# A hybrid decoder step: the MLP's down-projection computed by Strassen's seven products, like its up-projection

## The chip, the cores and the metric

The kernel runs on one core of a Trainium2 chip. The metric is the device time of one execution in microseconds. Five engines share the core's on-chip memory SBUF: TensorE (PE, matmuls into PSUM), VectorE (DVE), ScalarE (ACT), GpSimd (POOL) and SyncE (SP, which here only issues DMAs). Each runs its own instructions strictly in the order of the program; semaphores make one wait for another.

## The reference, cut to what matters

One layer on 1024 prompt tokens and 8 sample tokens (1032 columns in the kernel), with model width 1024 and MLP width 4096, in float32:

```python
def hybrid_layer(x, p, ...):
    ...
    x = x + jnp.concatenate([o, sg.astype(x.dtype)], axis=-1) @ w_out
    x = x + jnp.square(jax.nn.relu(rms_norm(x, g_ff) @ w_up)) @ w_down
    x = x + (p @ w_ple) * jax.nn.sigmoid(rms_norm(x, g_ple) @ w_ple_gate)
    return x, new_hist, s_new.astype(x.dtype), vg
```

The change concerns the second line's `@ w_down` and what follows it: the norm before the gate needs the sum of squares of each whole column of the new x.

## The kernel before, in words

Activations are kept transposed: 128 rows of the model width by 1032 tokens, so X1 is eight tiles. Every float32 product is three passes of a rounded format: a value is split into `hi` (a cast on ACT, line 147) and `lo` (a subtraction on DVE, line 150), and PE computes hi·hi, lo·hi and hi·lo. `form` (line 157) makes the split weight of one 128x512 group in a ring of four (`wsp`).

The up-projection already uses Strassen's algorithm: the two halves of the model width, of the hidden units and of each half of the tokens give 2x2 blocks, and seven products P1 to P7 of sums of blocks replace eight. `xform` makes the seven sums of the activations once and keeps them in FB. `up_stage` runs 16 pairs of hidden units, seven products each, each for two halves of the tokens with 12 matmuls of 258 columns (line 1175), and joins the products at their eviction from PSUM (lines 1186 to 1197). `hidden` takes relu and the square, splits the result (ACT 1206 and 1209, POOL 1210, DVE 1211) and writes it to DRAM (h_d, line 1212).

The down-projection is straight. `down` takes groups of two or four blocks of 128 hidden units (DBLK), loads their split activations back from h_d (`load_h`), and for each of eight output blocks and three token blocks (384, 384 and 264 columns) runs 3 matmuls per hidden block (lines 196 to 198). `evd` multiplies the PSUM sum by the norm's factor rr on DVE (line 1338) and adds it into X1 on POOL (line 1340). In the last group the addition is on DVE, `split_gain` (ACT 153, DVE 154) makes the gate's split input, and `add_ss` squares on ACT (line 1309) and adds to the sum of squares ss on POOL (line 1310).

Then the gate: PE's order is written by generators (`weave` and `spawn`, with modelled times). `gate_units` runs the matmuls for token blocks 0 and 1, then 2; beside them `p_in` transposes the per-layer input (pT, lines 1372 to 1374), and `rows` takes the column sums of ss by matmuls against ones (ms, line 1106), the inverse root on DVE, one transpose (msT, line 1123) and a way through DRAM (row_d) to rr. Evictions of the gate are held until that row is there. `first_out` writes the chunks of 128 tokens of the first two blocks while the third runs; the last three chunks (6, 7 and the sample tokens) are normed and written after it.

PE and SP have an order written out by hand in the down stage; ACT, DVE and POOL are put in order by a scheduler with its own estimates when the kernel is built.

Of the kernel before, what the change touches and what calls it, by code (L numbers as in the profile page):

```python
# [17 lines left out]
P = 128  # L18
# [14 lines left out]
HB = NT // 4  # L33
QBLK = [(i * HB, HB) for i in range(4)]

STEPS = (("P1", 0, "A", True), ("P4", 6, "C", True), ("P5", 3, "D", True), ("P6", 5, "A", False),
         ("P7", 4, "B", True), ("P2", 2, "A", True), ("P3", 1, "D", False))
FREE = [x[1] for x in STEPS]

# [3 lines left out]
DBLK = (2, 2, 4, 4, 4, 4, 4, 4, 4)  # L43
# [38 lines left out]
def trunk_step_kernel(  # L82
# [62 lines left out]
    def split(dst_hi, dst_lo, src, hi_eng, lo_eng):  # L145
        if hi_eng is S:
            S.copy(dst_hi, src)  # L147
        else:
            hi_eng.tensor_copy(dst_hi, src)
        lo_eng.tensor_sub(dst_lo, src, f32(dst_hi))  # L150

# [112 lines left out]
    h_d = dram.tile([32, P, 2, NT], F32, name="h_d")  # L264
# [6 lines left out]
    with ExitStack() as mix:  # L271
# [469 lines left out]
        def gdn_out(h, z):  # L741
# [18 lines left out]
            for o, w in BLK:  # L760
                b = slice(o, o + w)
                split(RA[8 + 2 * h][:, b], RA[9 + 2 * h][:, b], z[:, b], S, V)
# [235 lines left out]
        with tc.manual_schedule(engines={mybir.EngineType.PE}):  # L998
# [13 lines left out]
            for o, w in BLK:  # L1012
                for h in range(NH):
                    split(RA[2 * h][:, o : o + w], RA[2 * h + 1][:, o : o + w], us[h][:, o : o + w], S, V)
# [5 lines left out]
            for m in range(KD):  # L1020
                SY.dma_start(X1[m], xfm_d[m])
# [39 lines left out]
        fst = ctx.enter_context(pool("fst"))  # L1061
        FB = fst.tile([P, 14, 8 * HB], F32R, name="fb")
        Q = fst.tile([P, 8, HB], F32, name="q8")

        def xform(k, tp):

            H2 = HB // 2
            cells = FB[:, 7 * tp : 7 * tp + 7, :]
            for s in range(2):
                q = Q[:, 4 * s : 4 * s + 4, :].rearrange("p a (b c) -> p (a b) c", b=2)  # L1070
                with tc.high_priority(2 * PRI):
                    for i in range(2):
                        x = X1[k + 4 * i][:, 2 * HB * tp : 2 * HB * tp + 2 * HB].rearrange("p (a b) -> p a b", a=2)
                        S.activation(q[:, 2 * i : 2 * i + 2], x[:, :, H2 * s : H2 * s + H2],
                                     AF.Copy, scale=gff[:, k + 4 * i : k + 4 * i + 1])
                    G.tensor_sub(q[:, 4:6], q[:, 0:1].to_broadcast([P, 2, H2]), q[:, 1:3])
                    G.tensor_sub(q[:, 6], q[:, 2], q[:, 4])
                    G.tensor_sub(q[:, 7], q[:, 3], q[:, 6])  # L1078
                    hi = cells[:, :, HB * k + H2 * s : HB * k + H2 * s + H2]
                    lo = cells[:, :, HB * (k + 4) + H2 * s : HB * (k + 4) + H2 * s + H2]  # L1080
                    S.copy(hi, q[:, 1:8])  # L1081
                    V.tensor_sub(lo, q[:, 1:8], f32(hi))
# [13 lines left out]
    x1p = ctx.enter_context(pool("x1p", side="right"))  # L1096
    rr = x1p.tile([P, NT], F32, name="rr")

    def tok_stat(ss, power, chunks=range(NU + 1), more=None):
# [4 lines left out]
        for c in chunks:  # L1104
            r = P if c < NU else TS
            PE.matmul(ps[:r, c : c + 1], lhsT=ss[:, c * P : c * P + r], rhs=ones[:, 0:1], start=True, stop=not more)
            if more:
                d = (c - more[1]) * P
                PE.matmul(ps[:r, c : c + 1], lhsT=more[0][:, d : d + r], rhs=ones[:, 0:1], start=False, stop=True)
        tok_power(tok, ps, power, chunks, more)  # L1110
        return tok

    def tok_power(tok, ps, power, chunks, fast=None):
        c0, c1 = chunks[0], min(chunks[-1] + 1, NU)
        V.tensor_scalar(tok[:, c0:c1], ps[:, c0:c1], 1.0 / D, EPS, op0=ALU.mult, op1=ALU.add)
        if chunks[-1] == NU:
            V.tensor_scalar(tok[:TS, 8:9], ps[:TS, 8:9], 1.0 / D, EPS, op0=ALU.mult, op1=ALU.add)
        if power != 1:
            (rsqrt_act if fast else rsqrt)(tp, tok[:, :], tok[:, :], "rp")

    def row_stat(tok, out, i, ps):

# [4 lines left out]
        SY.dma_start(out, row_d[i, :NT].partition_broadcast(P))  # L1127
# [4 lines left out]
    th = ust.enter_context(pool("th", 2, side="right"))  # L1132
# [27 lines left out]
    def up_stage():  # L1160
        source = up_forms()
        forms = [next(source) for _ in range(RING)]
        for p in range(16):
            bank, u1, u2, u3 = {}, {}, {}, {}
            turn = TURN if p else TURN0
            for n, (i, t) in enumerate(turn):
                name, f, b, first = STEPS[i]
                wh, wl = forms[7 * p + i]
                if first:
                    bank[b, t] = pu.tile([P, 512], F32, tag=f"{b}{t}", name=b)[:, :HB]  # L1170
                ps = bank[b, t]
                x = FB[:, 7 * t + f, :].rearrange("p (j k c) -> p j k c", j=2, c=HB)
                for k in range(4):
# [3 lines left out]
                    if k < 3:  # L1177
                        yield 3 * HB * 0.000455
                if (i, t) not in turn[n + 1 :] and (i, 1 - t) not in turn[n + 1 :]:
                    forms += [w for w in (next(source, None),) if w]  # L1180
                q = Q[:, 4 * t : 4 * t + 4, :]
                with tc.high_priority(PRI):
                    if name == "P1":
                        u1[t] = tp.tile([P, HB], F32, tag="u1", name="u1")
                        S.copy(u1[t], ps)
                    elif name == "P6":
                        u2[t] = tp.tile([P, HB], F32, tag="u2", name="u2")
# [322 lines left out]
```

## Time and profile before

| | us |
|---|---|
| median of 3 runs (least to greatest) | 1430.12 (1429.49 to 1434.62) |
| the profiled execution: time, span of its instructions | 1426.78, 1425.1 |
| PE busy in the span | 1345.1 (94%) |
| from the end of the up-projection to msT | 907.8 to 1301.4 |
| of this, the stretch in which the down-projection runs | 920.1 to 1283.9 |
| gate and output, from msT to the end | 1301.4 to 1425.1 |

The last three rows are stretches on the span's clock, read from the trace. PE is the busiest engine; POOL and DVE are busy about half and six tenths of the span. TensorE's granted clock is given as a share of full speed.

### The profile page before, as it was taken

How to read it: one execution, taken by the hardware profiler on the slowest of the kernel's cores; microseconds unless marked ns; L12 is line 12 of the kernel's file. 1: busy time of each engine (PE TensorE's matmuls, PEld its weight loads, DVE VectorE, ACT ScalarE, POOL GpSimd, SP SyncE). 2: the span in 40 equal slices, each digit the busy share in tenths (PEclk: the TensorE clock that was granted, in tenths of full speed). 3: DMA queues.
4: the chain of work that ended last, by engine and by line, in shares of the span. 5: the costliest groups of instructions: out<-in, count | busy, mean ns of one | idle time of the engine just before them, and what ended most of it. 6: DMA issues, size and time to landing. Idle time of an engine off the chain costs nothing.

```text
span 1425.1 us, 25172 instructions
## 1 busy us (share of the span) xinstructions
PE 1345.1 (94%) x9567; PEld 1316.0 (92%) x9567; DVE 875.1 (61%) x1670; ACT 569.9 (40%) x1248; POOL 711.2 (50%) x798
## 2 busy tenths in 40 slices
PE   6979978989999899899999999699999999999998
PEld 4979968889899899799999999699999999998998
DVE  7745755375937846576776677475445445596346
ACT  6575645532233216555555454311111111154445
POOL 5300988847415306656656444296444445343331
PEclk9999989999999999999999999899999999999999
DMA  7334525555426721254445543674333344211124
GB/s 238 95 90 132 152 78 144 178 153 152 138 75 205 221 66 30 78 161 163 144 157 164 188 152 124 247 267 153 134 135 134 138 153 153 77 45 47 59 60 164
DMA packets 194837, 193.91 MB, mean 136 GB/s; under 512 B 18112, under 2 KB 160651, under 8 KB 190612
## 3 DMA queue, kind: packets, MB, share of 16 engines
q1 hardware_dynamic: 194716, 192.31, 42.0%
q8 instruction: 75, 1.23, 0.4%
q14 instruction: 46, 0.38, 0.1%
HBM read 131.76 MB, written 60.62 MB: 135 GB/s over the span
## 4 chain that ended last, share of the span: by engine, by line
PE 73%; POOL 9%; DVE 7%; DMA 4%; ACT 4%; issue 2%; SPq 0%; DVEq 0%; POOLq 0%; ACTq 0%
PE g L196 14%; PE g L198 14%; PE g L197 14%; PE A L1175 9%; PE D L1175 7%; PE B L1175 3%; PE C L1175 3%; POOL xinv L630 3%; POOL it L629 3%; DVE x L1340 1%; DVE fb L154 1%; DVE wlo L150 1%; POOL q L1078 1%; DMA s<-in_state_gdn 1%; DMA fb<-h_d 1%
## 5 line engine op out<-in xcount | busy, mean ns | idle before, releaser
L196 PE MATMUL g<-fb,whi 128*128 128x384 f32 (+1 forms) x960 | 309.6, 322 | 11.5 <-DMA fb<-h_d 11.0
L197 PE MATMUL g<-fb,wlo 128*128 128x384 f32 (+1 forms) x960 | 308.3, 321 | 0.0
L198 PE MATMUL g<-fb,whi 128*128 128x384 f32 (+1 forms) x960 | 307.7, 320 | 0.0
L196 PE MATMUL g<-ra,whi 128*128 128x384 f32 (+2 forms) x800 | 271.5, 339 | 0.6 <-ACT ra L374 0.6
L198 PE MATMUL g<-ra,whi 128*128 128x384 f32 (+2 forms) x800 | 255.5, 319 | 1.3 <-DVE ra L375 0.6
L197 PE MATMUL g<-ra,wlo 128*128 128x384 f32 (+2 forms) x800 | 254.4, 318 | 0.0
L1340 POOL TENSOR_TENSOR x<-x,t 128x384 f32<-128x384 f32 (+1 forms) x192 | 182.2, 960 | 143.4 <-DVE t L1338 143.3
L147 ACT CAST whi<-st 128x512 fp32r<-128x512 f32 x160 | 98.7, 620 | 349.4 <-PE g L198 336.8
L1338 DVE TENSOR_TENSOR t<-g,rr 128x384 f32<-128x384 f32 (+1 forms) x216 | 111.0, 515 | 148.2 <-PE g L198 140.1
L196 PEld LDWEIGHTS g<-fb,whi 128*128 128x128 f32 x960 | 181.5, 189 | 12.8 <-issue 10.3
L150 DVE TENSOR_TENSOR wlo<-st,whi 128x512 fp32r<-128x512 f32 x158 | 148.6, 941 | 61.4 <-ACT whi L147 57.8
L198 PEld LDWEIGHTS g<-fb,whi 128*128 128x128 f32 x960 | 181.4, 189 | 0.0
L197 PEld LDWEIGHTS g<-fb,wlo 128*128 128x128 f32 x960 | 181.4, 189 | 0.0
L196 PEld LDWEIGHTS g<-ra,whi 128*128 128x128 f32 x800 | 153.5, 192 | 2.8 <-ACT ra L374 1.0
L198 PEld LDWEIGHTS g<-ra,whi 128*128 128x128 f32 x800 | 153.1, 191 | 3.1 <-POOL ra L375 2.0
L197 PEld LDWEIGHTS g<-ra,wlo 128*128 128x128 f32 x800 | 153.9, 192 | 0.7 <-DVE wlo L150 0.3
L1175 PE MATMUL A<-fb,whi 128*128 128x258 f32 x768 | 147.8, 284 | 6.0 <-ACT fb L1081 4.6
L1175 PEld LDWEIGHTS A<-fb,whi 128*128 128x128 f32 x768 | 122.7, 190 | 7.0 <-ACT fb L1081 5.0
L1210 POOL TENSOR_TENSOR q<-q 128x516 f32<-128x516 f32 x64 | 69.3, 1086 | 103.4 <-ACT hs L1209 96.8
L1211 DVE TENSOR_TENSOR hs<-q,hs 128x516 fp32r<-128x516 f32 x64 | 87.1, 1360 | 46.8 <-POOL q L1210 46.7
L1175 PE MATMUL A<-fb,wlo 128*128 128x258 f32 x384 | 108.7, 283 | 0.0
L1175 PE MATMUL D<-fb,whi 128*128 128x258 f32 x512 | 98.7, 284 | 0.0
(382 smaller groups left out, 2596.8 us busy)
## 6 DMA issues: line engine op xcount, KB each, us to landing
h_d<-hs SPq DMA_DIRECT2D x64, 516.0 KB
fb<-h_d SPq DMA_DIRECT2D x32, 1032.0 KB
st<-in_w_down SPq DMA_DIRECT2D x32, 512.0 KB
st<-in_w_in SPq DMA_DIRECT2D x24, 512.0 KB
ck<-ck_d SPq DMA_DIRECT2D x32, 320.0 KB
ra<-in_w_up SPq DMA_DIRECT2D x32, 256.0 KB
rb<-in_w_up SPq DMA_DIRECT2D x32, 256.0 KB
st<-in_w_ple_gate SPq DMA_DIRECT2D x16, 512.0 KB
```

The source lines that it names most:

```text
L147: S.copy(dst_hi, src)
L150: lo_eng.tensor_sub(dst_lo, src, f32(dst_hi))
L196: PE.matmul(ps[:, :w], lhsT=whi[k], rhs=xh, start=(k == 0), stop=False)
L197: PE.matmul(ps[:, :w], lhsT=wlo[k], rhs=xh, start=False, stop=False)
L198: PE.matmul(ps[:, :w], lhsT=whi[k], rhs=xl, start=False, stop=(k == nk - 1))
L629: G.tensor_mul(tv, a, x)
L630: G.tensor_sub(X[:, j + 1 :, :w], X[:, j + 1 :, :w], tv)
L1175: PE.matmul(ps, lhsT=a[:, k, :], rhs=x[:, c, k, :], start=(first and k == 0 and j == 0), stop=(k == 3 and j == 2), skip_group_check=True)
L1210: G.tensor_mul(q, q, q)
L1211: V.tensor_sub(v[:, 1], q, f32(v[:, 0]))
L1338: V.tensor_mul(t[:, :w], ps[:, :w], rr[:, o : o + w])
L1340: (V if last else G).tensor_add(xv, xv, t[:, :w])
```

## The change

The hidden activations are no longer split before they go to DRAM. The up-projection's eviction writes relu² of a 2x2 group of blocks, `dforms` makes the other four of the seven sums with three POOL instructions, and two DMAs write the seven unsplit forms to f_d (4 groups of 1024 hidden units by 7 forms). Tokens lie in quarters of 256, 256, 260 and 260 columns for this, so X1 is loaded in three pieces each, and the forms of the up-projection lie in two tiles, which makes the copy and the subtraction of `xform` two instructions each. X1 is saved to x1_d, and its memory, FB's and Q's are given up after the up-projection.

`down` then goes through 4 row groups of w_down by 7 products (DSTEPS gives the order P1, P5, P6, P7, P4, P2, P3). A product is 4 output blocks by 2 halves by 12 matmuls of 256 or 260 columns; its form comes by one load of 1 MB into `raw` and is split by ACT and DVE (`split_raw`), and its weights are quarters of w_down in SBUF, summed on POOL where the product wants a sum, and then split. Seven sums per output block are kept in SBUF (ACC and three more): the first group's products are copied there by ACT, those of the others are added by DVE. In the last group these are joined: 20 additions on POOL and 8 on DVE (`add`), then `finish`: the product with rr on DVE, X1 (reloaded from x1_d) added on POOL, the square on ACT into one tile `sq`, the sum of squares on POOL. The gate's input for quarters 0 and 2 is made as the sums become final; that for quarters 1 and 3, which needs memory of the loop, after it. The gate runs in four blocks, 0 and 2 and then 1 and 3; four chunks are written beside the second pass and five after it. The load of w_ple and of the per-layer input stands after the loop's last activations.

```diff
-DBLK = (2, 2, 4, 4, 4, 4, 4, 4, 4)
+DSTEPS = (("P1", 0), ("P5", 4), ("P6", 5), ("P7", 6), ("P4", 3), ("P2", 1), ("P3", 2))
...
-    h_d = dram.tile([32, P, 2, NT], F32, name="h_d")
+    f_d = dram.tile([4, 7, P, 8 * 258], F32, name="f_d")
+    x1_d = dram.tile([KD, P, NT], F32, name="x1_d")
...
             for m in range(KD):
-                SY.dma_start(X1[m], xfm_d[m])
+                for dst, src in permuted(X1[m], xfm_d[m], 0, NT):
+                    SY.dma_start(dst, src)
...
+        FB = [(fst.tile([P, 4, 4128], F32R, name="fb"), 3), (fst.tile([P, 3, 4128], F32R, name="fa"), 0)]
...
+                    for fb, i0 in FB[::-1]:
+                        hi, lo = fb[:, :, c0 : c0 + h2], fb[:, :, c0 + 4 * w : c0 + 4 * w + h2]
+                        qi = q[:, i0 : i0 + fb.shape[1]]
+                        S.copy(hi, qi)
+                        V.tensor_sub(lo, qi, f32(hi))
...
+                        V.tensor_add(q[:, 3], u2[t], ps)
+                if name in ("P7", "P3"):
+                    for func in (AF.Relu, AF.Square):
+                        v = q[:, 1:3] if name == "P7" else q[:, 0:4:3]
+                        S.activation(v, v, func)
+                if name == "P3":
+                    dforms(p, t, q)
+                yield 3 * w * 0.000455
+    def dforms(p, t, q):
+        w = WT[t]
+        tt = tp.tile([P, 4 * 260], F32, tag="tt", name="tt")[:, : 4 * w].rearrange("p (a b) -> p a b", a=4)
+        G.tensor_sub(tt[:, 1:4:2], q[:, 3:4].to_broadcast([P, 2, w]), q[:, 0:3:2])
+        G.tensor_sub(tt[:, 2], q[:, 2], tt[:, 1])
+        G.tensor_sub(tt[:, 0], q[:, 1], tt[:, 2])
+        c0 = 1024 * t + w * (p % 4)
+        SY.dma_start(f_d[p // 4, 0:3, :, c0 : c0 + w].rearrange("f p c -> p f c"), q[:, 0:3])
+        SY.dma_start(f_d[p // 4, 3:7, :, c0 : c0 + w].rearrange("f p c -> p f c"), tt)
...
+        for m in range(KD):
+            SY.dma_start(x1_d[m], X1[m])
+            yield 3.0
...
+    ACC = pacc.tile([P, 2, 2, 4, 516], F32, name="acc")
+    ss = pacc.tile([P, 2, 516], F32, name="ss")
+    sq = pacc.tile([P, 516], F32, name="sq")
...
+    seq = [(j, i) for j in range(4) for i in range(7)]
...
+    def load_raw(n):
+        if n < len(seq):
+            j, i = seq[n]
+            SY.dma_start(raw, f_d[j, DSTEPS[i][1]])
+    def split_raw(n):
+        if n < len(seq):
+            hi, lo = HC[n % 2]
+            with tc.high_priority(PRI):
+                for c in (slice(0, 1024), slice(1024, 2064)):
+                    S.copy(hi[:, c], raw[:, c])
+                    V.tensor_sub(lo[:, c], raw[:, c], f32(hi[:, c]))
...
+    def down_forms():
+        for j in range(4):
+            sums = dst.tile([P, 4, 4, P], F32, tag="s", name="sums")
+            for name, _ in DSTEPS:
+                for p in range(4):
+                    with tc.high_priority(PRI):
+                        if name == "P5":
+                            G.tensor_add(sums[:, p], a_of("A21", p), a_of("A22", p))
+                        elif name == "P6":
+                            G.tensor_sub(sums[:, p], sums[:, p], a_of("A11", p))
+                        if name in ("P7", "P3"):
+                            f = dst.tile([P, 4, P], F32, tag="t", name="sd")
+                            G.tensor_sub(f, *((a_of("A21", p), a_of("A11", p)) if name == "P7" else (a_of("A12", p), sums[:, p])))
+                        else:
+                            f = {"P1": "A11", "P4": "A22", "P2": "A12"}.get(name)
+                            f = a_of(f, p) if f else sums[:, p]
+                        f = form(f)
+                    yield f
...
+    def finish(ab, nn, p, xo):
+        a = ACC[:, ab, nn, p]
+        V.tensor_mul(a, a, rr[:, nn])
+        G.tensor_add(a, a, xo[:, p])
+        if nn in begun:
+            S.activation(sq, a, AF.Square)
+            G.tensor_add(ss[:, nn], ss[:, nn], sq)
+        else:
+            begun.add(nn)
+            S.activation(ss[:, nn], a, AF.Square)
+    def gate_in(ab, nn, p):
+        m = p + 4 * ab
+        hi, lo = XS[ab, nn]
+        split_gain((hi[:, p], lo[:, p]), ACC[:, ab, nn, p], gple[:, m : m + 1])
...
+    def down():
+        load_raw(0)
+        load_a(0, "A11")
+        split_raw(0)
+        load_raw(1)
+        load_a(0, "A21")
+        load_a(0, "A22")
+        load_a(0, "A12")
+        row_get(rr, 1)
+        source = down_forms()
+        forms = [next(source) for _ in range(RING)]
+        xo = {}
+        for n, (j, i) in enumerate(seq):
+            name = DSTEPS[i][0]
+            split_raw(n + 1)
+            load_raw(n + 2)
+            hs = HC[n % 2]
+            end = j == 3
+            for p in range(4):
+                wh, wl = forms.pop(0)
+                for t in range(2):
+                    w = WT[t]
+                    ps = psd.tile([P, 512], F32, tag="d", name="d")[:, :w]
+                    xh, xl = (h[:, 1024 * t : 1024 * t + 4 * w].rearrange("p (k c) -> p k c", k=4) for h in hs)
+                    for k in range(4):
+                        PE.matmul(ps, lhsT=wh[:, k, :], rhs=xh[:, k, :], start=(k == 0), stop=False)
+                        PE.matmul(ps, lhsT=wl[:, k, :], rhs=xh[:, k, :], start=False, stop=False)
+                        PE.matmul(ps, lhsT=wh[:, k, :], rhs=xl[:, k, :], start=False, stop=(k == 3))
+                    to = {"P2": "P1", "P3": "P6"}.get(name, name) if end else name
+                    a = acc[to][:, p, TOFF[t] : TOFF[t] + w]
+                    with tc.high_priority(PRI):
+                        if j == 0:
+                            S.copy(a, ps)
+                        else:
+                            V.tensor_add(a, a, ps)
+                f = next(source, None)
+                if f:
+                    forms.append(f)
+                if end:
+                    def add(eng, x, y):
+                        eng.tensor_add(acc[x][:, p], acc[x][:, p], acc[y][:, p])
+                    if name == "P6":
+                        add(G, "P6", "P1")
+                        add(G, "P1", "P2")
+                    elif name == "P7":
+                        add(G, "P7", "P6")
+                        add(G, "P6", "P5")
+                        add(V, "P5", "P7")
+                        add(G, "P6", "P3")
+                    elif name == "P4":
+                        add(V, "P7", "P4")
+                        finish(1, 1, p, xo[1, 1])
+                    elif name == "P2":
+                        finish(1, 0, p, xo[1, 0])
+                        gate_in(1, 0, p)
+                    elif name == "P3":
+                        finish(0, 0, p, xo[0, 0])
+                        gate_in(0, 0, p)
+                yield 24 * 258 * 0.000455
+            if not end:
+                for name in {3: ("A11", "A21"), 4: ("A22",), 6: ("A12",)}.get(i, ()):
+                    load_a(j + 1, name)
+            elif i == 3:
+                xo[1, 1] = x1_old("A11", 1, 1)
+                xo[1, 0] = x1_old("A21", 1, 0)
+            elif i == 4:
+                xo[0, 0] = x1_old("A22", 0, 0)
+            elif i == 5:
+                xo[0, 1] = x1_old("A11", 0, 1)
+        for p in range(4):
+            finish(0, 1, p, xo[0, 1])
...
+    for p in range(4):
+        for ab in range(2):
+            gate_in(ab, 1, p)
...
-        weave(gate_units((0, 1), False, None))
...
-        weave(gate_units((2,), True, q7))
+        weave(gate_units((0, 2)))
+        spawn(first_out(), FIN0)
...
+        weave(gate_units((1, 3), [q7]))
```

On POOL at the end of the down-projection, the order before is this (x1 is X1, ss the sum of squares, q a square):

```order
L1340 TENSOR_TENSOR x1_5547<-x1_5547,t_14154 128x384
L1340 TENSOR_TENSOR x1_5547<-x1_5547,t_14170 128x384
L1340 TENSOR_TENSOR x1_5547<-x1_5547,t_14186 128x264
L1310 TENSOR_TENSOR ss_11069<-ss_11069,q_14274 128x384
L1310 TENSOR_TENSOR ss_11069<-ss_11069,q_14295 128x384
```

POOL's last work for the loop is a single addition per eviction, and none of PE's operands are made there. In the changed kernel, this is POOL in the same place, inside the last row group (sd is a sum of weights that PE's products P7 and P3 wait for, acc the sums kept on chip, a11 and a21 old X1 or weights):

```order
L1363 TENSOR_TENSOR sd_14390<-a21_11058,a11_11061 128x512
L1437 TENSOR_TENSOR acc_11027<-acc_11027 128x516
L1437 TENSOR_TENSOR acc_11027<-acc_11027,acc_P2_11040 128x516
L1437 TENSOR_TENSOR acc_11027<-acc_11027 128x516 x2
L1363 TENSOR_TENSOR sd_14737<-a12_11055,sums_13873 128x512
L1437 TENSOR_TENSOR acc_11027<-acc_11027 128x516 x2
L1437 TENSOR_TENSOR acc_11027<-acc_11027,acc_P3_11041 128x516
L1437 TENSOR_TENSOR acc_11027<-acc_11027 128x516 x2
L1437 TENSOR_TENSOR acc_11027<-acc_11027,acc_P3_11041 128x516
L1383 TENSOR_TENSOR acc_11027<-acc_11027,a11_11061 128x516
```

The weight sums of the product P3 stand among the joining additions. Counted from the first of these (the first line with L1437 that the whole order of the last group has), 14 instructions stand before the first sum of P3 (sd_14737), and 43 before its fourth and last.

On ACT where the gate begins, the order before is:

```order
L153 ACTIVATE fb_6085<-x1_5547,vec_149 128x384
L1309 ACTIVATE q_14703<-x1_5547 128x384
L153 ACTIVATE fb_6085<-x1_5547,vec_149 128x264
L1309 ACTIVATE q_14724<-x1_5547 128x264
L1373 CAST fb_6085<-pT_14761 128x384
```

Each square follows its cast, and the casts of the per-layer input come when all squares are done. After (xt is the gate's input of quarters 1 and 3, wpl the split w_ple, pp the per-layer input):

```order
L166 ACTIVATE xt00_15030<-acc_11027,vec_150 128x516
L166 ACTIVATE xt10_15032<-acc_11027,vec_150 128x516
L150 CAST wpl00_15077<-st_15081 128x1024
L150 CAST wpl10_15079<-st_15085 128x1024
L1385 ACTIVATE sq_11029<-acc_11027 128x516 x2
L1543 CAST pp00_15089<-pT_15118 128x256
L1385 ACTIVATE sq_11029<-acc_11027 128x516
L1543 CAST pp10_15091<-pT_15129 128x256
L1385 ACTIVATE sq_11029<-acc_11027 128x516
```

Eight casts of the gate's input (the last two are shown) and two of w_ple now stand before the last six squares, and casts of the per-layer input among these.

## Rows read from the trace of the kernel before

**Rows 1.** The page: the span, and busy time, share and count of each engine.

```profile
span 1425.1 us, 25172 instructions
PE 1345.1 (94%) x9567; PEld 1316.0 (92%) x9567; DVE 875.1 (61%) x1670; ACT 569.9 (40%) x1248; POOL 711.2 (50%) x798
```

**Rows 2.** Busy time by stretch: the start of the down stage, its body, its last group, the wait for the gate's row, and the gate with the output.

```profile
core 0: us, PE busy (x) PEld busy (x) DVE busy (x) ACT busy (x) POOL busy (x), PEclk, DMA share, GB/s
907.80:920.10 12.30, 1.35 (x5) 0.85 (x4) 3.14 (x7) 3.06 (x6) 2.09 (x2) 0.71 0.98 339
920.10:1243.00 322.90, 322.90 (x2045) 322.83 (x2046) 170.00 (x254) 37.79 (x60) 182.24 (x192) 1.00 0.42 156
1243.00:1283.90 40.90, 40.50 (x259) 40.10 (x257) 38.77 (x63) 20.69 (x44) 17.44 (x16) 1.00 0.13 40
1283.90:1301.40 17.50, 14.10 (x75) 12.94 (x74) 13.95 (x33) 7.14 (x17) 5.34 (x5) 0.80 0.11 30
1301.40:1425.10 123.70, 117.61 (x782) 117.12 (x781) 58.34 (x115) 60.01 (x112) 35.23 (x36) 0.99 0.28 90
```

**Rows 3.** The chain that ended last, where the up-projection passes into the down-projection: start, duration, what.

```profile
902.09 2.87 PE A L1175 x24
904.96 2.87 PE D L1175 x24
...
907.85 0.42 DVE q L1197
...
910.35 9.67 DMA fb<-h_d
...
920.07 0.69 PE g L196
```

**Rows 4.** Durations by line on DVE, ACT and POOL: count, then least, median and greatest duration in ns, first and last start.

```profile
L150 DVE TENSOR_TENSOR wlo<-s,whi x64: 676/680/1804, 585.1 to 897.5; 128x512 fp32r<-128x512 f32 x64
L150 DVE TENSOR_TENSOR fb<-st,fb x2: 1226/1524/1823, 941.0 to 943.5; 128x1024 fp32r<-128x1024 f32 x2
L154 DVE SCALAR_TENSOR_TENSOR fb<-x,vec,fb x24: 482/618/1376, 1242.1 to 1293.0; 128x384 fp32r<-128x384 f32 x16, 128x264 fp32r<-128x264 f32 x8
L1195 DVE TENSOR_TENSOR q<-u,A x32: 407/418/424, 599.5 to 905.0; 128x258 f32<-128x258 f32 x32
L1211 DVE TENSOR_TENSOR hs<-q,hs x64: 680/1488/1785, 600.9 to 913.9; 128x516 fp32r<-128x516 f32 x64
L1157 POOL TENSOR_TENSOR s<-rb,s x16: 1276/1291/1747, 591.8 to 895.1; 128x512 f32<-128x512 f32 x16
L153 ACT ACTIVATE fb<-x,vec x24: 499/616/620, 1241.5 to 1291.3; 128x384 fp32r<-128x384 f32 x16, 128x264 fp32r<-128x264 f32 x8
L147 ACT CAST fb<-st x2: 1042/1044/1047, 938.8 to 939.8; 128x1024 fp32r<-128x1024 f32 x2
```

**Rows 5.** The timeline of DVE and of POOL in the up stage: start, duration, instruction.

```profile
706.65 1.68 DVE L1211 TENSOR_TENSOR hs<-q,hs 128x516 fp32r<-128x516 f32 x1
710.85 1.23 DVE L1211 TENSOR_TENSOR hs<-q,hs 128x516 fp32r<-128x516 f32 x1
...
706.47 1.31 POOL L1153 TENSOR_TENSOR s<-rb,ra 128x512 f32<-128x512 f32 x1 [0.63 <-DVE wlo L150]
711.49 1.75 POOL L1157 TENSOR_TENSOR s<-rb,s 128x512 f32<-128x512 f32 x1
```

**Rows 6.** The same at the end of the down stage, and PE's matmuls there (their starts give the time of one).

```profile
1282.24 1.04 POOL L1310 TENSOR_TENSOR ss<-ss,q 128x384 f32<-128x384 f32 x1 [1.91 <-ACT q L1309]
1291.49 2.15 POOL L1310 TENSOR_TENSOR ss<-ss,q 128x384 f32<-128x384 f32 x2 [1.56 <-ACT q L1309]
...
1282.32 1.38 DVE L1340 TENSOR_TENSOR x<-x,t 128x384 f32<-128x384 f32 x1
...
1283.31 0.28 PE L197 MATMUL g<-fb,wlo 128*128 128x264 f32 x1
1283.80 0.28 PE L198 MATMUL g<-fb,whi 128*128 128x264 f32 x1
1292.68 2.41 PE L1106 MATMUL ms<-ones,ss 128*128 128x1 f32 x12 [1.86 <-POOL ss L1310]
1301.37 0.28 PE L1123 MATMUL msT<-ident,tok 128*9 128x128 f32 x1
1302.72 0.34 PE L197 MATMUL g<-fb,wlo 128*128 128x384 f32 x1
1303.25 0.34 PE L197 MATMUL g<-fb,wlo 128*128 128x384 f32 x1
```

**Rows 7.** DMA issues on SP at the start of the down stage, and output halves on ACT and DVE at the end of the program: start, duration, instruction.

```profile
908.39 0.57 SPq L1279 DMA_DIRECT2D st<-in_w_down  x1
...
1419.00 1.82 ACT L1402 ACTIVATE yo<-yT,tok 128x512 f32<-128x512 f32 x3 [0.95 <-DVE tok L252]
...
1420.42 0.64 DVE yo L1404
```

More of the change, by code (lines that the diff above doesn't have):

```diff
@@ L1103, in tok_stat, with row_put @@
         V.memset(tok, 1.0)
[L1104 to L1110, printed above, removed]
-        return tok
[L1113 to L1121, printed above, removed]
+        tok_sums(ps, ss, chunks, more)
+        tok_mean(tok, ps, chunks)
+        (rsqrt_act if more else rsqrt)(tp, tok[:, :], tok[:, :], "rp")
+        return tok
+    def row_put(tok, i, ps):
         PE.transpose(ps[:9, :], tok, ident)
@@ new lines, in trunk_step_kernel @@
+    for name in ("A22", "A21"):
+        AC[name] = dl.tile([P, 2064], F32, name=name.lower())
+    HC[0] = [dl.tile([P, 2064], F32R, name=f"h0{i}") for i in range(2)]
+    AC["A11"] = dl.tile([P, 2064], F32, name="a11")
+    raw = dl.tile([P, 2064], F32, name="raw")
+    seq = [(j, i) for j in range(4) for i in range(7)]
[10 more added lines that the diff above has]
+                    V.tensor_sub(lo[:, c], raw[:, c], f32(hi[:, c]))
@@ L1249, in trunk_step_kernel @@
+    with tc.manual_schedule(engines={mybir.EngineType.PE, mybir.EngineType.SP}):
+        weave(down())
+    dx.close()
+    dlx.close()
+    gst = ctx.enter_context(pool("gst"))
+    XS.update({(ab, 1): [gst.tile([P, 4, 516], F32R, name=f"xt{ab}{i}") for i in range(2)] for ab in range(2)})
+    for p in range(4):
+        for ab in range(2):
+            gate_in(ab, 1, p)
     tp = ctx.enter_context(pool("tp", 3, side="right"))
     wst2 = ctx.enter_context(pool("wst2", side="right"))
-    ss = wst2.tile([P, NT], F32, name="ss")
@@ L1290, in halves @@
             with tc.high_priority(PRI):
-                ready.append([form(x) for x in staged[n]])
+                ready.append([form(staged[n][:, 4 * j : 4 * j + 4, :]) for j in range(2)])
+    stage()
+    stage()
+    halves()
     cur = [0]
@@ L1357, in trunk_step_kernel @@
         SY.dma_start(st, w_ple[0, k * P : (k + 1) * P, :])
-        split(wpl[k][0], wpl[k][1], st[:, :], S, V)
-    pp = [cell(4 + k) for k in range(2)]
+        split(wpl[k][0][:, :], wpl[k][1][:, :], st[:, :], S, V)
+    pp = [[gst.tile([P, 2, 516], F32R, name=f"pp{k}{i}") for i in range(2)] for k in range(2)]
     pt = []
@@ L1443, in rows, with first_out @@
             ev()
-    def first_out(c1):
-        tok = tok_stat(ss, -0.5, range(c1))
+    first, second = (0, 1, 4, 5), (2, 3, 6, 7, NU)
+    def first_out():
+        tok = tok_stat(ss, first)
         yield FIN
-        for c in range(c1):
-            while c >= c1 - LATE and not gated:
+        for c in first:
+            while c == first[-1] and not gated:
                 yield 0.5
```

371 lines of the change are left out of this document (197 added, 174 removed).

## The prediction

> **What bounds the kernel now.** I read the page first: PE is busy 94% of the span, POOL 50%, DVE 61% [rows 1]. The busy time by stretch shows where this holds. In the body of the down stage PE has no idle time at all (322.90 of 322.90 us), beside 170 us of DVE and 182 us of POOL. At its start PE works 1.35 us in 12.3 us, at a granted clock of 0.71 and a DMA share of 0.98; after its end it waits for the sum of squares (14.10 us busy in 17.5 us, clock 0.80) [rows 2]. So fewer matmuls shorten the body, as long as DVE, POOL and ACT keep up; each thing that PE waits for at the two ends counts in full. The stretch to compare is from the last matmul of the up-projection, 907.8 us (904.96 + 2.87, [rows 3]), to msT, 1301.4 us [rows 6]: 393.6 us. Then I read durations by line for the new work [rows 4], and the timelines where DVE and POOL meet [rows 5, 6].
>
> **The change part by part.** The up-projection gains nothing and loses little: it goes on being a run of PE. POOL's squaring and DVE's subtraction of `hidden` go, three POOL subtractions and two DMAs per half come, beside PE. X1's loads become 24 issues instead of 8: 16 more at 0.57 us [rows 7] are at most 9 us if all lie on the path, nothing if beside other loads; I take 1.
>
> *Products.* 24 matmuls of 258 columns take 2.87 us, 0.12 each [rows 3], so a product of the new loop, 96 of such a width, takes 11.52 us, and 28 of them 322.6 us. Before, the body and last group are 363.8 us [rows 2]. On PE alone this saves 41 us.
>
> *Start.* Before, 12.3 us [rows 2]. After, the first product's activations and weights can be loaded before the up-projection ends, since their memory comes free eight half products (11.5 us) earlier; but raw for the second product, A21 and A22 (3 MB) stand on SP behind the last two form stores, which come 5 to 6 us after the end of up. At 339 GB/s [rows 2] 3 MB are 9 us, with landing and two splits some 19 to 24 us after the end, less the 11.5 us of the first product: 8 to 13 us. Bounds: 4 us, if only DVE's backlog after the last eviction counts (0.42, a split of 1.23 and two of 0.68, a cast of 1.04, [rows 3, 4]), and 20 if the first product waits for the stores as well. I take 12, nearest to the row of before.
>
> *The 23 products ahead of P6 of the last group.* 23 x 11.52 = 265 us if PE bounds. DVE has per product 2 splits of 1.23, 4 of 0.68 and, from the second group on, 8 additions of 0.42 from PSUM [rows 4]: 8.5 of 11.5 us. POOL has 16 sums of 1.29 in a group of seven products, 2.9 us per product, of which DVE must stand aside for at most the whole: 11.4. This is close; the cover is the ring of four weights, and I take no loss, with an upper bound of 1 us in each of the 16 products with DVE additions.
>
> *Last group from P6.* PE needs 5 x 11.52 = 57.6 us. Here the joining lies, and it is not free. What POOL does from there: 8 sums for P7 and P3, 20 joining additions, 16 of X1, 14 of squares: 58 instructions. What DVE does with two inputs in SBUF: 8 halves of splits, 21 weight splits, 8 additions, 16 products with rr, 16 gate splits, and the two of w_ple.
>
> DVE with two SBUF inputs and POOL don't run side by side. The 0.68 us subtraction that began at 706.65 ended at 708.33, 0.55 us after POOL's 706.47 + 1.31; POOL's 1.29 us subtraction that began at 711.49, inside DVE's of 710.85 to 712.08, ended 1.16 us after it [rows 5]. At the end of the down stage DVE's addition of 1282.32 ended 0.42 us after POOL's of 1282.24 [rows 6]. In each some 0.13 us is overlapped, and the rest adds. The line's medians say the same: 1488 ns for DVE's subtraction that met POOL, 680 least; the addition from PSUM keeps 407 to 424 [rows 4].
>
> So the pair works off a sum. POOL: 58 x 1.16 = 67.3 us (additions of 516 taken as those of 512). DVE: splits 8 x 1.10 = 8.8, weights 21 x 0.55 = 11.6, additions 8 x 0.55 = 4.4, products 16 x 0.55 = 8.8, gate splits 16 x 0.64 = 10.2 (0.482 and 0.618 at 264 and 384 columns give an estimate of 0.77 at 516, less 0.13), w_ple 2 x 1.10 = 2.2: 46.0. Together 113 us instead of 57.6. PE feels it inside the group: P3's last weight sum is POOL's 44th instruction there, 44 x 1.16 = 51 us, beside about 35 us of DVE's, so at about 86 us, where PE wants it 54.7 us after the start. PE stands some 31 us. Bounds: 58 x 1.29 = 75 us if POOL never waits, and 130 if nothing overlaps at all (below). I take 113, by the two collisions, plus 4 for the end of the chain: eight casts (0.62 at 384 columns) and two of w_ple (1.04) stand on ACT before the last six squares, all squares share one tile `sq`, and PE's transposes of the per-layer input stand in order before the column sums and wait for loads behind w_ple's split.
>
> The Trainium skill, "SBUF — State Buffer", section "Who interferes with whom", speaks against this change: a DVE instruction with two SBUF inputs contends with a GpSimd instruction that reads SBUF, the loser is blocked fully, and one with at most one SBUF input doesn't contend. The trace agrees in kind, and shows that some 0.13 us of each still overlaps.
>
> *From the sum of squares to msT:* 1292.7 to 1301.4, 8.7 us [rows 6], kept.
>
> Sum: 12 + 265 + 113 + 4 + 8.7 = 402.7 against 393.6: 9.1 us more. Ahead of msT PE had done 42 matmuls of the gate at 0.176 (7.4 us); now 48 at 0.12 (5.8): 1.6 more is left. Four blocks need 24 x 4 x 0.12 = 11.52 us per output block instead of 24 x (2 x 0.176 + 0.122) = 11.38 [rows 6]: eight times, with a quarter more for the per-layer product, 1.4. After the last matmul five chunks are left instead of three: two times two halves at 0.61 to 0.64 on ACT and DVE together [rows 7], 1.3, and 1 MB more at some 340 GB/s, 3 us; I take 3. With X1's loads, 9.1 + 1.6 + 1.4 + 3 + 1 = 16.1. The profiled execution took 1426.8 us (span 1425.1 and 1.7 around it): 1443. The median of the runs is 3.3 us above it: 1446.
>
> **The rivals.**
> (1) *The pair costs nothing, PE's saving remains: faster.* If POOL's additions run at 1.29 us without DVE's delay, the last group is 75 + 3 us to the first eviction, 78, so 39 less than my 117: 1407. For it: POOL's own additions in the down stage, x<-x, keep pace with PE, and a part of DVE's work (its PSUM additions, 17 us) can lie under POOL's. Against: three collisions, each added. It decides if the last group takes under 93 us, where it begins to be faster by 0.5%.
> (2) *Nothing overlaps.* POOL 58 x 1.29 = 75 us, DVE 8 x 1.23 + 21 x 0.68 + 8 x 0.68 + 16 x 0.68 + 16 x 0.77 + 2.5 = 55, together 130: 17 more, 1463. Against: the 0.55 and 1.16 us. By the rule of the Trainium skill's page taken at its word, full blocking, this would be the time.
> (3) *DVE bounds the loop from the second group on.* 16 products of 12.5 instead of 11.5 us: 1462. For it: 11.4 of 11.5 us, in-order queues, and POOL's sums bunched in four of seven products. Against: the sums and the additions from PSUM can lie side by side.
> (4) *The gains balance.* Start at 6 instead of 12, and half of DVE's 46 us placed where POOL waits for its operands anyway: the pair 113 - 12, together 18 less: 1428.
>
> **How the numbers follow.** Forecast 0.34 (1437 to 1455 by itself), rival 1 0.23, rival 2 0.12, rival 3 0.13, rival 4 0.18. What a measurement of this kernel can tell from no change is about 0.5%, 7 us: slower is above 1437.3, faster under 1423.0. Slower: 0.34 + 0.12 + 0.13, less 0.01 that falls under the bound, 0.58; within: rival 4 and the edges, 0.20; faster 0.22. The range reaches from the upper end of rival 1's half (a last group of 83 us) to both slow ones: 1411 to 1467.
>
> **What would show it.** In the changed kernel, DVE's subtractions and POOL's additions in the last group with medians well above 0.68 and 1.29; PE idle there some 30 us or more, released by the split of P3's weights; the first column sums some 117 us after the start of P6. The three groups before it with PE busy at least 97%. The start: first to second product about 12 us of idle time. I am wrong if POOL's additions are at 1.3 us and PE doesn't stand in P3, if PE stands in the second and third group, or if the clock falls in the gaps and the matmuls after them take twice as long in more than a few microseconds.

## The result, and the profile after

The changed kernel takes 1450.99 us (median of 4 runs, 1448.22 to 1452.77), the kernel before, run beside it, 1430.15: 1.0137 times as long, with a 95% interval of 1.0111 to 1.0164. It is slower, by 21 us; the forecast was 1446. PE's busy time fell, and the span grew: the page of the changed kernel begins

```profile
span 1450.0 us, 26432 instructions
PE 1322.1 (91%) x10195; PEld 1292.2 (89%) x10195; DVE 892.5 (62%) x1719; ACT 676.9 (47%) x1427; POOL 709.6 (49%) x723
```

beside 1345.1 (94%) for PE in [rows 1]. Where the time went is read from the busy time by stretch, with the stretches cut as in [rows 2]: from the up-projection's end to the first matmul, to the last gap at the second product's start, the 22 products up to P6 of the last group, the matmuls from P6 on, the wait for the gate's row, and the rest.

```profile
core 0: us, PE busy (x) PEld busy (x) DVE busy (x) ACT busy (x) POOL busy (x), PEclk, DMA share, GB/s
916.30:920.60 4.30, 0.03 (x2) 0.02 (x1) 1.94 (x2) 4.11 (x7) 3.74 (x4) 1.00 0.53 186
920.60:940.40 19.80, 14.67 (x100) 14.06 (x101) 9.54 (x10) 7.54 (x15) 9.08 (x7) 0.83 0.85 296
940.40:1190.80 250.40, 250.40 (x2104) 250.40 (x2104) 182.31 (x261) 113.29 (x182) 82.37 (x54) 1.00 0.42 148
1190.80:1287.90 97.10, 69.89 (x489) 67.75 (x488) 90.50 (x101) 29.78 (x44) 77.23 (x48) 0.84 0.28 93
1287.90:1321.90 34.00, 14.27 (x83) 13.41 (x81) 18.20 (x40) 14.96 (x28) 15.64 (x10) 0.70 0.21 62
1321.90:1450.00 128.10, 120.33 (x1019) 119.62 (x1016) 63.07 (x148) 64.55 (x136) 32.75 (x42) 0.99 0.28 88
```

The third row is the whole gain: PE without a gap for 250 us. The fourth is the loss. 480 matmuls that need 57.6 us take 97.1: 27 us of that are idle, and in the rest PE is busy 69.9 us, some 12 more than the work needs, and the mean granted clock of the stretch is 0.84. Its second part, and in it the longest gap, show how the clock falls:

```profile
1225.00:1287.90 62.90, 36.96 (x216) 35.43 (x217) 62.20 (x68) 17.56 (x27) 47.55 (x31) 0.76 0.23 76
1262.80:1273.00 10.20, 5.45 (x24) 5.23 (x24) 10.20 (x10) 3.94 (x6) 7.78 (x6) 0.50 0.00 0
```

From 1262.8 to 1273.0 the granted clock is 0.50, the level of 1.2 GHz; PE had been idle since 1259.5 and works again at 1267.6. From 1225.0 to 1287.9 DVE is busy 62.2 of 62.9 us, so PE isn't what bounds this part. The view of waits of 1205 to 1290 us names who ended the idle time (engine, line, releaser: us, times, longest):

```profile
PE d L1422 <- DVE wlo L153: 26.9, 9, 8.1
PE d L1421 <- ACT whi L150: 0.3, 1, 0.3
```

PE waits for the second half of a split weight, made on DVE. The longest of these waits are below, with the DVE instruction behind each; sd is a weight sum made on POOL, for P3, and a is a quarter of w_down as it was loaded, for P2.

```profile
1251.55 0.58 PE L1422 MATMUL d<-h,wlo 128*128 128x256 f32 x1 [4.60 <-DVE wlo L153]
1267.55 0.58 PE L1422 MATMUL d<-h,wlo 128*128 128x256 f32 x1 [8.08 <-DVE wlo L153]
1278.93 0.58 PE L1422 MATMUL d<-h,wlo 128*128 128x256 f32 x1 [5.85 <-DVE wlo L153]
...
1250.82 0.68 DVE L153 TENSOR_TENSOR wlo<-a,whi 128x512 fp32r<-128x512 f32 x1
1265.86 1.64 DVE L153 TENSOR_TENSOR wlo<-sd,whi 128x512 fp32r<-128x512 f32 x1
1278.19 0.68 DVE L153 TENSOR_TENSOR wlo<-sd,whi 128x512 fp32r<-128x512 f32 x1
```

What DVE and POOL do there is seen in the groups by shape, from P6's start to the column sums (count, busy, mean ns of one, idle time ahead and its releaser):

```profile
L1382 DVE TENSOR_TENSOR acc<-acc,rr 128x516 f32<-128x516 f32 x16 | 22.5, 1409 | 0.0
L153 DVE TENSOR_TENSOR wlo<-a,whi 128x512 fp32r<-128x512 f32 x8 | 11.0, 1388 | 0.0
L167 DVE SCALAR_TENSOR_TENSOR xs<-acc,vec,xs 128x516 fp32r<-128x516 f32 x8 | 10.8, 1356 | 0.0
L1430 DVE TENSOR_TENSOR acc<-acc,d 128x260 f32<-128x260 f32 x17 | 7.1, 416 | 1.8 <-PE d L1423 1.7
...
L1383 POOL TENSOR_TENSOR acc<-acc,a 128x516 f32<-128x516 f32 x16 | 25.4, 1586 | 8.8 <-DVE acc L1382 8.8
L1437 POOL TENSOR_TENSOR acc<-acc 128x516 f32<-128x516 f32 x12 | 21.1, 1764 | 10.3 <-DVE acc L1430 10.3
```

A DVE instruction that takes 0.68 us alone [rows 4] takes 1.4 here, POOL's 1.29 becomes 1.6 to 1.8, and the additions from PSUM keep their 0.41. This is the collision of [rows 5], through the whole group. The tail is in the chain that ended last (start, duration, what), where the last squares and their additions take turns behind a load:

```profile
1299.23 1.15 DVE wpl L153
1300.39 3.79 DMA pt<-in_p_prompt
1304.23 0.70 PE pT L1540 x2
1304.95 0.37 ACT pp L1543
1305.33 0.54 ACT sq L1385
1305.94 1.29 POOL ss L1386
...
1312.00 1.28 POOL ss L1386
1313.33 2.27 PE ms L1129 x14
```

The column sums begin at 1313.33, 122.5 us after P6's start at 1190.8, and msT stands at 1321.86.

### The profile page after: what moved, and what is told of

The parts are those of the page before. It is cut to its first block, busy times and chain, and to the rows that moved or that the text cites. A ratio compares the mean times of both kernels' runs of the same rounds, so it can differ in the third digit from the quotient of the medians.

```text
span 1450.0 us, 26432 instructions
## 1 busy us (share of the span) xinstructions
PE 1322.1 (91%) x10195; PEld 1292.2 (89%) x10195; DVE 892.5 (62%) x1719; ACT 676.9 (47%) x1427; POOL 709.6 (49%) x723
## 4 chain that ended last, share of the span: by engine, by line
PE 68%; POOL 10%; DVE 10%; ACT 4%; DMA 3%; issue 3%; SPq 1%; DVEq 0%; POOLq 0%; ACTq 0%
PE A L1209 9%; PE D L1209 6%; PE d L1422 6%; PE d L1423 6%; PE d L1421 6%; PE g L209 5%; PE g L211 4%; PE g L210 4%; PE B L1209 3%; PE C L1209 3%; POOL xinv L644 3%; POOL it L643 3%; PE g L1613 2%; PE g L1615 2%; PE g L1614 2%
## 5 line engine op out<-in xcount | busy, mean ns | idle before, releaser
L1422 PE MATMUL d<-h,wlo 128*128 128x260 f32 (+1 forms) x896 | 258.9, 289 | 30.7 <-DVE wlo L153 30.7
L209 PE MATMUL g<-ra,whi 128*128 128x384 f32 (+3 forms) x800 | 274.4, 343 | 1.2 <-ACT ra L388 1.0
L1421 PE MATMUL d<-h,whi 128*128 128x260 f32 (+1 forms) x896 | 257.8, 288 | 5.9 <-ACT whi L150 5.9
L211 PE MATMUL g<-ra,whi 128*128 128x384 f32 (+3 forms) x800 | 257.6, 322 | 0.8 <-POOL ra L389 0.4
L1423 PE MATMUL d<-h,whi 128*128 128x260 f32 (+1 forms) x896 | 257.7, 288 | 0.0
L210 PE MATMUL g<-ra,wlo 128*128 128x384 f32 (+3 forms) x800 | 256.6, 321 | 0.0
L1422 PEld LDWEIGHTS d<-h,wlo 128*128 128x128 f32 x896 | 174.5, 195 | 33.1 <-DVE wlo L153 33.1
L1421 PEld LDWEIGHTS d<-h,whi 128*128 128x128 f32 x896 | 173.9, 194 | 6.5 <-ACT whi L150 6.5
L1423 PEld LDWEIGHTS d<-h,whi 128*128 128x128 f32 x896 | 174.2, 194 | 0.0
L153 DVE TENSOR_TENSOR wlo<-st,whi 128x512 fp32r<-128x512 f32 x94 | 74.6, 794 | 46.5 <-ACT whi L150 45.1
L1339 DVE TENSOR_TENSOR h<-raw,h 128x1024 fp32r<-128x1024 f32 (+1 forms) x56 | 79.6, 1429 | 28.6 <-ACT h L1338 28.6
L1209 PE MATMUL A<-fb,whi 128*128 128x260 f32 (+1 forms) x512 | 97.0, 282 | 0.0
L1236 ACT ACTIVATE q<-q 128x520 f32<-128x520 f32 (+1 forms) x128 | 78.4, 631 | 25.3 <-DVE q L1232 19.8
L644 POOL TENSOR_TENSOR xinv<-xinv,it 32x31 f32<-32x31 f32 (+15 forms) x124 | 80.9, 653 | 9.6
```

What stands on the lines that cost most here:

```text
L209: PE.matmul(ps[:, :w], lhsT=whi[k], rhs=xh, start=(k == 0), stop=False)
L210: PE.matmul(ps[:, :w], lhsT=wlo[k], rhs=xh, start=False, stop=False)
L211: PE.matmul(ps[:, :w], lhsT=whi[k], rhs=xl, start=False, stop=(k == nk - 1))
L644: G.tensor_sub(X[:, j + 1 :, :w], X[:, j + 1 :, :w], tv)
L1209: PE.matmul(ps, lhsT=a[:, k, :], rhs=x[:, c, k, :], start=(first and k == 0 and j == 0), stop=(k == 3 and j == 2), skip_group_check=True)
L1236: S.activation(v, v, func)
```

## The experiments

Times are medians of the runs, or one execution where no interval is given; the ratio is to the kernel before, run beside it. P6's start is taken 251.9 us after the start of the second product, as in the changed kernel (1190.8 - 938.9). P6's own first matmul comes some 0.8 us after that in the changed kernel, E3, E5, E6 and E8, but 2.3 us after it in E2 and E4: there TensorE's granted clock was at 0.50, the level of 1.2 GHz, for 3.4 us right after the idle time at the second product's start. E2's row:

```profile
937.10:940.50 3.40, 3.40 (x18) 3.40 (x17) 3.14 (x3) 1.79 (x5) 3.40 (x3) 0.50 0.44 175
```

So beside the others the last column is 1.5 us too long for E2 and E4.

| | us | ratio to before | P6 to column sums |
|---|---|---|---|
| changed kernel | 1450.99 | 1.0137 (1.0111 to 1.0164) | 122.5 |
| E1 tokens in order | 1451.5 | 1.0151 (1.0124 to 1.0179) | |
| E2 additions on DVE | 1435.6 | 1.0025 (1.0005 to 1.0044) | 108.9 |
| E3 own tiles | 1448.35 | 1.0119 (1.0102 to 1.0135) | 120.0 |
| E4 all | 1428.47 | 0.9976 (0.9962 to 0.999) | 95.4 |
| E5 products from PSUM | 1439.48 | | 110.9 |
| E6 own tiles, sums earlier | 1442.0 | 1.0067 (1.005 to 1.0084) | 110.6 |
| E7 one tile of forms | 1452.23 | | |
| E8 no joins | 1403.65 | | 74.6 |

**E5: the disputed cost by itself.** DVE's 16 products with rr read a constant tile in PSUM in place of the sum.

```diff
-        V.tensor_mul(a, a, rr[:, nn])
+        V.tensor_mul(a[:, :512], no, rr[:, nn, :512])
```

> The changed kernel in which the 16 products with rr take a constant tile in PSUM instead of the sum (512 of 516 columns), so DVE has one input in SBUF there; the sums' product is left out, and the loop has 7 PSUM buffers instead of 8. Theory (the pair excludes): these 16 instructions go from a mean of 1.41 us to 0.6 to 0.7, POOL's additions beside them lose their delay, and the column sums come 10 to 20 us sooner after P6's start than 122.4. Rival (the last group is a chain of engines that wait for each other's results, whatever the port): the instructions take what they took, or the sums come at 120 us or later.

The line in E5's groups by shape:

```profile
L1385 DVE TENSOR_TENSOR acc<-no,rr 128x512 f32<-128x512 f32 x16 | 10.5, 677 | 0.1
```

677 ns instead of 1409, and the column sums 11.6 us sooner. The operation, its engine and its place stayed; only one operand left SBUF (the width lost four columns, the loop one of its eight PSUM buffers). The neighbours that kept two inputs in SBUF kept means of 0.9 to 1.7 us. One part of the expectation failed: POOL's additions of X1 stayed long, 1.66 us in the mean for 1.59, with such neighbours still beside them; what went is their wait for the product, 8.8 us before and none now. E5 also takes away the product's read of the sum; E2, which keeps it, closes that gap: there the same line with both inputs in SBUF takes 681 ns once POOL has only its weight sums to do. So the long durations are the pair's, and the chain of results isn't what holds the group.

**E2: the additions on DVE.**

```diff
-                        add(G, "P6", "P1")
+                        add(V, "P6", "P1")
...
-        G.tensor_add(a, a, xo[:, p])
+        V.tensor_add(a, a, xo[:, p])
...
-            G.tensor_add(ss[:, nn], ss[:, nn], sq)
+            V.tensor_add(ss[:, nn], ss[:, nn], sq)
```

> The changed kernel with the 20 joining additions, 16 additions of X1 and 14 of squares (in all 50 of the last group's additions) moved from POOL to DVE; POOL keeps its 8 weight sums. Theory: DVE with two inputs in SBUF and POOL exclude each other, so an addition costs the pair 0.55 to 0.68 us on DVE instead of 1.16 on POOL: from P6 of the last group DVE needs 55 us for what it had, 50 x 0.68 = 34 for the new, 17 for its additions from PSUM, less 8 that come after the sums, some 98 us; the column sums come 95 to 108 us after P6's start instead of 122.4, the time is 14 to 25 us less. Rival: DVE's long instructions in the last group (1.4 to 1.7 us) are not POOL's doing: 50 more of them on the engine with the most to do take 70 us, and the time is 20 us or more greater.

E2's groups by shape, the same stretch:

```profile
L1383 DVE TENSOR_TENSOR acc<-acc,a 128x516 f32<-128x516 f32 x16 | 12.5, 789 | 0.0
L1437 DVE TENSOR_TENSOR acc<-acc 128x516 f32<-128x516 f32 x16 | 10.8, 685 | 0.1
L1382 DVE TENSOR_TENSOR acc<-acc,rr 128x516 f32<-128x516 f32 x16 | 10.7, 681 | 0.0
L1386 DVE TENSOR_TENSOR ss<-ss,sq 128x516 f32<-128x516 f32 x14 | 9.7, 690 | 2.6 <-ACT sq L1385 2.1
```

50 instructions more for the busier engine, and its products with rr are back at 0.68: 13.6 us less to the sums by the table (15.1 from P6's own start), 15.4 us less in all. The rival, that DVE is slow there by itself, would have lengthened it. The sums came at the late end of what was expected (95 to 108), and the tail's order, which stayed, fits that: a wait of 17.1 us of PE's transposes for the load of the per-layer input is still in E2's view of waits.

**E3 and E6: the order of the tail.** E3 gives the squares a second tile and w_ple's load tiles of its own.

```diff
-    dl.tile([P, 1032], F32, name="gap")
+    gap = dl.tile([P, 1032], F32, name="gap")
+    sqs = [sq, gap[:, :516]]
...
-            S.activation(sq, a, AF.Square)
-            G.tensor_add(ss[:, nn], ss[:, nn], sq)
+            q = sqs[p % 2]
+            S.activation(q, a, AF.Square)
+            G.tensor_add(ss[:, nn], ss[:, nn], q)
...
-        st = ty.tile([P, D], F32, tag="yo", bufs=2, name="st")
+        st = ty.tile([P, D], F32, tag="wp", bufs=2, name="st")
```

> The changed kernel with two tiles for the squares instead of one (the second in a gap of the memory plan) and with tiles of their own for w_ple's load, so that the per-layer input is loaded without waiting for w_ple's split; in the built order all squares then stand ahead of the gate's casts. Theory: the 25 us from the last matmul of the loop (1287.9) to the column sums (1313.3) are partly a wait on ACT's order (late load, transposes, casts, then squares): the sums come some 10 us earlier, the time is 8 to 13 us less. Rival: POOL and DVE bound that stretch anyhow: less than 3 us.

Only 2.6 us less. The size is the rival's, the reason is neither's: the sum of squares was ready 11 us earlier after P6's start, and PE's timeline shows a new wait ahead of the column sums (in brackets the idle time and what ended it).

```profile
1297.46 1.27 POOL L1388 TENSOR_TENSOR ss<-ss,gap 128x516 f32<-128x516 f32 x1
...
1307.01 3.54 PE L1129 MATMUL ms<-ones,ss 128*128 128x1 f32 x16 [17.17 <-DVE pp L1546]
```

The sums end at 1298.7, the matmuls that want them begin at 1307.0. Four transposes of the per-layer input stood ahead on PE and held all four PSUM buffers; DVE, in order, emptied them only behind eight splits of the gate's input and two of w_ple. E6 puts the column sums behind two transposes.

```diff
-        yield ROW
+        yield 4.0
...
-        spawn(rows(), ROW0)
+        spawn(rows(), 1.0)
```

> The changed kernel (additions on POOL as it has them) with the two tiles for the squares, the own tiles for w_ple's load and the column sums behind two transposes instead of four. With the first two alone the sum of squares was complete at 1298.7 us, yet the column sums began at 1307.0, behind a transpose that waited for a PSUM buffer. Theory: that wait goes, the column sums come within 1 us of the last addition on POOL, 5 to 8 us sooner than with the first two edits alone, and the time is 1440 to 1444 us. Rival: the gate's preparation on DVE is what the gate then waits for: 1446 us or more.

1442.0 us, as expected; the sums come 9.4 us sooner than in E3, more than the 5 to 8 expected. PE now follows POOL's last addition at once: sums at 1298.02 after an addition that ended at 1297.96. So the tail's order was worth 9 us of the changed kernel. Part of this is the pair's work put elsewhere: DVE's eight splits of the gate's input and two of w_ple, 9.0 us, which stood ahead of the last squares, come after the sums in E3 and E6.

**E4: both together.**

> The kernel with all 50 additions of the last group on DVE, with the two tiles for the squares and the own tiles for w_ple's load, and with the column sums put on PE behind two transposes of the per-layer input instead of four (in the runs before, four transposes took all PSUM buffers and the sums waited for DVE to empty one). Theory: what is left of the last group is DVE's work alone, and the tail's order no longer adds: the column sums come 96 to 102 us after P6's start, against 108.7 with the additions on DVE alone; the time is 1424 to 1431 us, at or under the kernel before. Rival: the gate's own preparation (eight splits, w_ple's splits, the per-layer input), now behind the sums, holds the gate up by as much: 1433 to 1437 us.

PE's timeline of E4:

```profile
1278.38 1.01 PE L1129 MATMUL ms<-ones,ss 128*128 128x1 f32 x4 [9.04 <-DVE ss L1388]
1281.39 2.72 PE L1129 MATMUL ms<-ones,ss 128*128 128x1 f32 x12 [2.00 <-DVE ss L1388]
1294.18 0.27 PE L1150 MATMUL msT<-ident,tok 128*9 128x128 f32 x1 [1.14 <-DVE tok L254]
```

The sums come 27 us sooner than in the changed kernel (some 28.6 from P6's own start), and the whole interval of the ratio, 0.9962 to 0.999, lies under 1: the seven products beat the straight loop by 0.1 to 0.4%. The straight loop's own tail was not put in order for this comparison, so no run here tells what both would be with the same care. A part goes back as the rival said: msT follows 12.8 us after the sums instead of 8.5, because the gate's preparation now stands between.

**E8: nothing to join.** The joining additions, products, additions of X1 and of squares are left out.

```diff
-                        eng.tensor_add(acc[x][:, p], acc[x][:, p], acc[y][:, p])
+                        pass
...
-        V.tensor_mul(a, a, rr[:, nn])
-        G.tensor_add(a, a, xo[:, p])
...
-            G.tensor_add(ss[:, nn], ss[:, nn], sq)
```

> The changed kernel without the 28 joining additions, the 16 products with rr, the 16 additions of X1 and the 14 of squares: these are left out, the splits, weight sums, squares and the gate's splits stay. It measures what the new loop takes when its last group has nothing to join. Theory: PE bounds the whole loop then: the last group's matmuls take 57 to 62 us instead of 97, the column sums come 60 to 75 us after P6's start (the tail's order stays), the time is 1390 to 1405 us, so that the joining cost 45 to 60 us and more than ate the 41 us of matmuls that the seven products save. Rival: splits and additions from PSUM keep PE waiting without any joining: the last group takes 75 us or more, the time is 1415 us or more.

E8's last group, by stretch:

```profile
1190.60:1248.20 57.60, 57.60 (x486) 57.60 (x486) 46.36 (x80) 31.76 (x48) 9.06 (x7) 1.00 0.50 166
```

PE has no gap: 57.6 us, as its matmuls alone need. The time is 47 us under the changed kernel's. So the splits, weight sums and additions from PSUM are hidden, and the joining is what isn't.

**E1 and E7: the front.** E1 leaves the tokens in their old order, E7 makes the forms of the up-projection one tile again.

```diff
-        c = min(o + w, 768)
...
+        return [(dst[:, o : o + w], src[:, o : o + w])]
```

> The changed kernel with the tokens left in their old order: X1 is loaded with one DMA per tile (8 instead of 24) and the splits ahead of the output projection are single again. The quarters then hold other tokens than the rest of the kernel takes them for, so the values differ and the work doesn't. In the changed kernel the first matmul of the up-projection comes at 580.6 us, before the change at 572.6. Theory: the loads and splits in pieces cause this: the first matmul at 573 to 575, the time 6 to 8 us less. Rival: the two-piece split of the up-projection's forms, or the order of earlier work, causes it: first matmul at 579 to 582, the time within 2 us of the changed kernel.

```diff
-        FB = [(fst.tile([P, 4, 4128], F32R, name="fb"), 3), (fst.tile([P, 3, 4128], F32R, name="fa"), 0)]
+        FB = [(fst.tile([P, 7, 4128], F32R, name="fb"), 0)] * 2
...
-                    for fb, i0 in FB[::-1]:
+                    for fb, i0 in FB[:1]:
```

> The changed kernel with the up-projection's forms in one tile again, cast and subtracted in one instruction each. Two places are looked at. Start of the down stage: the memory of the first product's activations and weights comes free only with the last matmul of the up-projection; theory: the first matmul of the down stage comes 10 to 16 us after the up-projection's end instead of 4.6, the 23 products after it 4 to 10 us later in all. Rival: loads aren't what the start waits for: within 2 us. Start of the up-projection: in all runs of the changed kernel it comes 221.4 to 221.8 us after the last inverse step on POOL, before the change 218.1; if the two-piece split costs that, this one shows 218 to 219.5, if not 221 to 222.

E1 is the rival's: first matmul at 579.1 us, time unchanged, and counted from the last inverse step on POOL it comes after 221.5 us for 221.8, so X1's 16 more loads cost at most 0.3 us there. Its first matmul of the up-projection still waits as in the changed kernel, whose timeline of PE has these rows at the start of the two stages:

```profile
580.60 0.36 PE L1209 MATMUL A<-fa,whi 128*128 128x256 f32 x1 [1.75 <-DVE x L1058]
...
920.58 0.39 PE L1421 MATMUL d<-h,whi 128*128 128x256 f32 x1 [4.27 <-ACT whi L150]
```

The first matmul of the down stage in E7:

```profile
922.77 0.58 PE L1421 MATMUL d<-h,whi 128*128 128x256 f32 x1 [9.52 <-ACT whi L150]
```

In E7 the wait of 1.75 us for DVE is gone, but its up-projection starts 221.2 us after the last inverse step, against 221.8, and ends 557.4 us after it, against 557.6 (553.3 before the change): by the values set for E7, the two-piece split isn't what costs the time. The down stage's first matmul comes 9.5 us after the up-projection's end in E7, just under the 10 to 16 expected and 5.2 us later than in the changed kernel; 2.2 us of that are left at the loop's end, where 4 to 10 were expected for the 23 products: the early loads help, though less than thought.

## Why the prediction was right, point by point

- *Products: right.* 22 products in 250.4 us without a gap, 11.4 each for 11.52, and DVE at 182 of 250 us. The rival that DVE bounds the loop falls.
- *Start: right in size, not in place.* The forecast of 12 us was a wait between the first and the second product. The first matmul came 4.3 us after the up-projection's end, 3.1 us of idle time lie inside the first product, and only 2.0 between the two; matmuls at a mean granted clock of 0.83 (the second row by stretch) add the rest. The start and the 23 products took 274.5 us (916.3 to 1190.8), for 12 + 265 = 277, so that the agreement is partly luck.
- *The pair of DVE and POOL: right, and shown.* In 115.0 of the 122.5 us from P6's start to the column sums a two-input instruction of DVE or an instruction of POOL is running (counted from the trace), for the 113 of the sum. E5 shows the cause and E2 the remedy. The rule of the Trainium skill ("SBUF — State Buffer", section "Who interferes with whom") names the same two kinds of instruction, and E5 agrees with its other half, that one SBUF input doesn't contend: 677 ns. Rival 1, at 1407, falls. Rival 2, with 130, was 15 us too long.
- *PE's stall: right in size, half right in place.* 27 us for 31, but only 14.9 of them (8.1, 5.9 and 1.0) were released by splits of P3's weights, as named. 11.2 were released by splits of P4's and P2's weights, which need no sum of POOL: they stood on DVE behind its long instructions.
- *A sign of being wrong that came.* The prediction called itself wrong if the clock fell in the gaps and the matmuls after them took twice as long in more than a few microseconds. It fell, and PE's matmuls from P6 on took some 12 us more than the 57.6. The sum has no term for this and held all the same, as DVE was busy 62.2 of the 62.9 us in which most of it happened; how much of it reached the end, no run shows.
- *The end of the chain: the term that was too small.* "Plus 4" measured 7.5, what is left of the 122.5 us beside the pair's 115.0. From the end of w_ple's first split (1300.4) it is 13 us to the column sums, but 8.6 of these are POOL's last squares, which the 113 counts already; between them POOL waits for ACT and the late load, as named.
- *Up to the up-projection's start: 8.0 us late, forecast 1.* X1's loads weren't it (E1). 4.3 us are there already at the last inverse step on POOL (358.8 us for 354.5), in a part that the change touches only by four of X1's loads: over the traces of the eight experiments it varies from 354.3 to 358.4. The remaining 3.7 are steady (221.2 to 222.6 in all traces against 218.1). By E7 the two-piece split isn't the cause; it stays open.
- *Gate and output: 4.4 us longer* (128.1 for 123.7), forecast 6.0 with the 1.6 of matmuls left over.

In rival 4 the working has a slip: half of DVE's 46 us is 23, not 12, and would give 1417 for 1428. It bears on no other number.

The forecast of 16 us in the profiled execution came out as 24.9 in spans: in the main 7.0 more than forecast ahead of the up-projection, 5.5 more from P6 to the column sums, and 2.5 and 1.6 less at the start and in the gate. The medians differ by 21 us, as the profiled execution before was 3.3 us faster than its median. The step that decides the sign holds, with a smaller price than the 55 us of the sum (113 for 57.6): 47 us lost by the joining (E8) stand against the 41 that PE was to save. Without the joining the kernel is at 1404, with it at 1451.

## What to carry to other kernels

Fewer matmuls pay only where the additions that replace them fit beside PE. Here they were hidden in three groups and exposed in the last, where everything that joins the products comes due at once and PE's own operands queue among it. When DVE is busy with two-input work, giving its additions to POOL doesn't relieve it: count both engines' two-input instructions as one queue, put the work on the faster of the two, or let one operand come from PSUM. And after one wait is removed, look at what stands next in order on the engine that waited: E3's gain of 11 us on POOL was lost to a transpose.

## What the runs showed of the hardware

That the busier of two engines can take work over and finish sooner: DVE got 50 additions more, and the stretch became some 15 us shorter (E2), as 0.69 to 0.89 us of DVE replaced 1.6 to 1.8 us of POOL and DVE's products went from 1.41 to 0.68. And the first 355 to 359 us of the program, with the same instructions in the changed kernel and in E2, differ by 4.5 us between these two traces, which is more than some terms of such a forecast.
